# The passage between sublayers of an encoder kernel, reordered by token halves

## The chip, the cores and the metric

One Trainium2 chip, of which one core runs the kernel. The metric is the device time of one execution, in microseconds (us); the median of three runs stands for a kernel.

## The reference, cut to what matters

Two layers with two sublayers each, on 256 tokens of width 2048, all in float32. A sublayer is `x = x + rms_norm(f(rms_norm(x, pre)), post)`, where `f` is a token mixer or a gated MLP with a short convolution:

```
for i in range(DEPTH):
    h = rms_norm(x, p['mix_pre'])
    m = mixer_dilated_gqa(h, ...) if i % 2 == 0 else mixer_mla(h, ...)
    x = x + rms_norm(m, p['mix_post'])
    h = rms_norm(x, p['ffn_pre'])
    x = x + rms_norm(conv_glu(h, ...), p['ffn_post'])
```

So there are four sublayers: mixer 0, FFN 0, mixer 1, FFN 1. The last thing that each of them does is a projection to 2048 columns, its norm, and the addition to `x`; the first thing that the next one does is a projection of the new `x`.

## The kernel before, in words

**Weights.** Every weight is cut into chunks of 128 x 1024 floats, listed in the order of their use (`all_chunks`, L949). SyncE loads a chunk into one of four `raw` buffers (`_load`, L99). `_split` (L106) then makes two parts of it, so that float32 products can be made of products of a shorter type (F32R): ACT copies the chunk to `whi` (L117), and DVE subtracts that from the chunk and writes the rest to `wlo` (L118). There are three buffers of each. `weights` (L129) hands out the next chunk and splits some chunks ahead.

**Inputs.** The input of a sublayer stands in SBUF with features on the partitions: 16 slices k of 128 features, each as a high part and a low part of 256 tokens, side by side. Four tiles `xhl[c]`, c = 0 to 3, hold four slices each (`split`, L319). The parts of one slice are made by one ACT instruction (L516) and one DVE instruction (L517) in `parted_by`, which also multiply by the gain of the norm before. The norm's other factor comes in later, so the square sums of the new `x` (`pre_norm`, L288) aren't needed at once.

**Projections.** `proj_t` (L176) gives features by tokens: for each chunk, which covers two slices k, eight pairs of products, one of 512 columns (the high weights by both parts of x, L186) and one of 256 (the low weights by the high part, L187), into four PSUM banks. `proj_tok` (L191) gives tokens by features: for each chunk and each token half t six products of 512 columns (`mm3`, L172 to L174). The FFN begins with `proj_t`, mixer 1 with `proj_tok`. PSUM has two sets of four banks, tagged `acc` and `at`; both kinds of projection write to `acc` first, the transposes to `at`.

**The passage.** `out_proj` (L332) computes the four blocks of 512 columns of a sublayer's result. Of the last block the last three chunks (`HOLD`) are held: all of token half 0 is finished with them, then all of half 1. When a half is through, `factor(t)` (L369) takes its square sum and root on ACT (L282, L374) and four small steps on DVE (L375 to L379); `add` (L381) adds the scaled result to `x` on DVE. `scaled` (L349) multiplies a block by the norm's gains on DVE. Then TensorE transposes the new `x` (`turns`, L400), 32 transposes of 128 x 128 in all (L405), in pairs of slices that share a PSUM bank, and the parts of each slice are made. The first pair of slices is done at once, the other seven one by one as the next sublayer asks for weights (`rest`, L438, through `follow`, L142). `warm` (L151) puts products of zeros into TensorE's queue, ten and three for each passage. The first chunk of the next sublayer is split in the midst of it (L411). All this runs three times; after the last sublayer (`pre is None`) the result goes out instead.

**What sets the order.** The framework places the instructions on each engine: it goes by its own model of what is ready when, and by the program's order where several are. `behind` puts instructions after a given one on that one's engine; here the seven later pairs and, through `gate`, the splits of weights come behind the first additions.

## Time and profile before

| | us |
|---|---|
| median of three runs | 2072.53 |
| lowest and highest | 2072.30, 2072.53 |
| the profiled execution, its own time | 2072.57 |
| its span in the profile | 2070.8 |

| engine | busy us | share of the span | instructions |
|---|---|---|---|
| TensorE, products (PE) | 2057.9 | 99% | 10977 |
| TensorE, weight loads (PEld) | 1764.1 | 85% | 10977 |
| VectorE (DVE) | 1340.6 | 65% | 2051 |
| ScalarE (ACT) | 1084.6 | 52% | 1695 |

The profile is of one execution. A row of a timeline has the start in us from the span's start, the us until its last instruction ends, the engine, the line of the kernel, what it writes and reads, and how many instructions it merges; in brackets stands how long the engine was idle before it, and what ended that. Products overlap, so a product's length is more than the distance to the next one. A row of groups has the busy time, the mean length in ns, and the idle time before. A row of windows has the stretch, its length, the busy time and instructions of PE, PEld, DVE, ACT and POOL, the granted clock of TensorE as a share of full speed, the share of the DMA engines, and GB/s. The three passages stand at about 323 to 357, 1058 to 1090 and 1323 to 1357 us.

### The profile page before, as it was taken

What the parts mean: (1) busy time and instruction counts of PE and PEld (TensorE: products, weight loads), DVE (VectorE), ACT (ScalarE), POOL (GpSimd) and SP (SyncE); (2) the same over time, 40 slices, a digit from 0 to 9 for tenths busy, and PEclk for the clock granted to TensorE, in tenths of its full rate; (3) what the DMA queues carried; (4) which work ended last, traced back from release to release, by engine and by line L of the source; (5) the groups of instructions that cost most, each with busy time, mean ns of one, the idle gap of its engine ahead of it and who ended that gap; (6) DMA issues with size and microseconds to landing.
All of it is one profiled execution on the core that took longest, in us unless ns stands there. A gap on an engine that the chain in (4) does not pass through costs nothing.

```text
span 2070.8 us, 28951 instructions
## 1 busy us (share of the span) xinstructions
PE 2057.9 (99%) x10977; PEld 1764.1 (85%) x10977; DVE 1340.6 (65%) x2051; ACT 1084.6 (52%) x1695; POOL 0.2 (0%) x4
## 2 busy tenths in 40 slices
PE   9999999999999999999999999999999999999998
PEld 7888888888888888888888998888888888888886
DVE  6877757667667667444466875666766766754444
ACT  6655546555555555344455654555555555544443
POOL 0000000000000000000000000000000000000000
PEclk9999999999999999999999999999999999999999
DMA  8545565666666666666665445566666666666664
GB/s 315 176 153 163 164 200 174 186 193 190 188 192 191 187 192 190 196 198 199 198 186 170 125 129 177 177 188 190 185 195 191 188 191 190 185 200 198 198 194 154
DMA packets 108716, 385.96 MB, mean 186 GB/s; under 512 B 12064, under 2 KB 12576, under 8 KB 108576
## 3 DMA queue, kind: packets, MB, share of 16 engines
q1 hardware_dynamic: 108288, 383.83, 60.6%
q8 instruction: 86, 1.41, 0.3%
q14 instruction: 54, 0.44, 0.1%
q10 hardware_dynamic: 288, 0.28, 0.0%
HBM read 381.96 MB, written 2.10 MB: 185 GB/s over the span
## 4 chain that ended last, share of the span: by engine, by line
PE 98%; DVE 1%; ACT 0%; DMA 0%; issue 0%; DVEq 0%; SPq 0%
PE ps L186 31%; PE ps L172 16%; PE ps L174 16%; PE ps L173 16%; PE ps L187 16%; PE ps L463 1%; PE ps L242 1%; DVE x L383 1%; PE ps L405 0%; DMA raw<-in_w_in 0%; PE ps L790 0%; DVE wlo L118 0%; ACT junk L282 0%; PE ps L238 0%; DVE xhl L517 0%
## 5 line engine op out<-in xcount | busy, mean ns | idle before, releaser
L118 DVE TENSOR_TENSOR wlo<-raw,whi 128x1024 fp32r<-128x1024 f32 (+1 forms) x710 | 867.9, 1223 | 672.1 <-ACT whi L117 670.4
L117 ACT CAST whi<-raw 128x1024 fp32r<-128x1024 f32 (+1 forms) x710 | 745.9, 1052 | 786.5 <-PE ps L174 417.5
L186 PE MATMUL ps<-xhl,whi 128*128 128x512 f32 x2816 | 978.6, 394 | 1.0 <-DVE xhl L517 1.0
L187 PE MATMUL ps<-xhl,wlo 128*128 128x256 f32 x2816 | 779.2, 277 | 0.0
L186 PEld LDWEIGHTS ps<-xhl,whi 128*128 128x128 f32 x2816 | 527.6, 188 | 123.2 <-DVE xhl L517 1.9
L187 PEld LDWEIGHTS ps<-xhl,wlo 128*128 128x128 f32 x2816 | 528.7, 188 | 1.1 <-DVE wlo L118 0.5
L172 PE MATMUL ps<-whi,gh 128*128 128x512 f32 x704 | 273.9, 389 | 0.0
L174 PE MATMUL ps<-whi,gl 128*128 128x512 f32 x704 | 273.9, 389 | 0.0
L173 PE MATMUL ps<-wlo,gh 128*128 128x512 f32 x704 | 273.9, 389 | 0.0
L174 PEld LDWEIGHTS ps<-whi,gl 128*128 128x128 f32 x704 | 132.2, 188 | 27.7
L173 PEld LDWEIGHTS ps<-wlo,gh 128*128 128x128 f32 x704 | 132.2, 188 | 27.4
L172 PEld LDWEIGHTS ps<-whi,gh 128*128 128x128 f32 x704 | 132.2, 188 | 27.1
L172 PE MATMUL ps<-whi,xhl 128*128 128x512 f32 x352 | 138.8, 396 | 1.3 <-ACT whi L117 1.2
L173 PE MATMUL ps<-wlo,xhl 128*128 128x512 f32 x352 | 137.6, 391 | 0.0
L174 PE MATMUL ps<-whi,xhl 128*128 128x512 f32 x352 | 137.1, 391 | 0.0
L172 PE MATMUL ps<-whi,oh 128*128 128x512 f32 x256 | 100.0, 390 | 0.0
L173 PE MATMUL ps<-wlo,oh 128*128 128x512 f32 x256 | 99.7, 389 | 0.0
L174 PE MATMUL ps<-whi,ol 128*128 128x512 f32 x256 | 99.6, 389 | 0.0
L247 ACT COPY half<-ps 128x256 f32<-128x256 f32 x176 | 65.0, 369 | 45.6 <-PE ps L186 36.0
L172 PEld LDWEIGHTS ps<-whi,xhl 128*128 128x128 f32 x352 | 66.0, 188 | 15.1 <-ACT whi L117 1.5
L174 PEld LDWEIGHTS ps<-whi,xhl 128*128 128x128 f32 x352 | 66.0, 188 | 13.9
L173 PEld LDWEIGHTS ps<-wlo,xhl 128*128 128x128 f32 x352 | 66.3, 188 | 13.4 <-DVE wlo L118 0.9
(186 smaller groups left out, 1584.9 us busy)
## 6 DMA issues: line engine op xcount, KB each, us to landing
raw<-in_w_up SPq DMA_DIRECT2D x352, 512.0 KB, 4.1
raw<-in_w_down SPq DMA_DIRECT2D x176, 512.0 KB, 4.2
raw<-in_w_in SPq DMA_DIRECT2D x88, 512.0 KB, 3.8
raw<-in_w_out SPq DMA_DIRECT2D x64, 512.0 KB, 3.9
gb<-in_post SPq DMA_DIRECT2D x16, 256.0 KB, 3.9
raw<-in_w_qn SPq DMA_DIRECT2D x8, 512.0 KB, 3.6
raw<-in_w_kn SPq DMA_DIRECT2D x8, 512.0 KB, 3.6
raw<-in_w_v SPq DMA_DIRECT2D x8, 512.0 KB, 3.6
```

The source lines that it names most:

```text
L117: self.nc.scalar.copy(hi[:, s], raw[:, s])
L118: self.nc.vector.tensor_tensor(out=lo[:, s], in0=raw[:, s], in1=hi[:, s].bitcast(F32), op=ALU.subtract)
L172: mm(ps, lh, rh, start=start, stop=False)
L173: mm(ps, lh, rl, start=False, stop=False)
L174: mm(ps, ll, rh, start=False, stop=stop)
L186: mm(out[i], hi[:, s], x(k), start=k == 0, stop=False)
L187: mm(out[i][:, :T], lo[:, s], x(k)[:, :T], start=False, stop=k == nk - 1)
L242: self.tc.keep_in_program_order(self.nc.tensor.transpose(out, x, self.ident))
L247: self.nc.scalar.copy(b, ps[:, T:])
L383: return nc.vector.scalar_tensor_tensor(out=x, in0=m[c][:, t, s], scalar=r[t], in1=x, op0=ALU.mult, op1=ALU.add)
L463: nc.tensor.matmul(ps[:, i, :], l, r, start=n == 0, stop=n == len(pairs) - 1))
```

## The change

The passage is written anew. What it does:

- The transposes of one slice have a PSUM bank of their own (`turn(k, t)`), where two slices shared one.
- The second half's held chunks get work between them (`between` in `proj_tok`): ahead of the first one the factor, the addition to the first block and the scaling of token half 0; ahead of the second the split of the next sublayer's first chunk; ahead of the third the transposes of slices 0 and 1 for half 0, their parts, and the first half of the second chunk's split (`middle`).
- The next sublayer's first chunk is computed by token halves: what concerns half 0 comes first, then `second()` (the transposes of slices 2 and 3 for half 0, the factor, addition and scaling for half 1, four transposes for half 1, the parts of slices 0 and 1 for half 1, the rest of the second chunk's split, the parts of slices 2 and 3), then half 1. In `proj_tok` that is only an order. In `proj_t` (`by_halves`) the eight pairs of 512 and 256 columns become sixteen of 256 and 128, the wider ones with two runs of 128 columns; the fourth tile's products come after `second()`.
- Both stretches stand in `strict()`: on TensorE, DVE and ACT each instruction is tied behind the one written before it.
- The products of zeros in the passage go away.
- The six later pairs, the next norm's square sums and the splits of weights come behind the half 1 parts of slice 1 on ACT and DVE.
- The scaled results lie two blocks to a tile, in `xm1` and `xm2`; `xhl[1]` is put into `xm3`, `xhl[2]` into `xm1`, `xhl[3]` into `xm2`.

```
+    def _pieces(self, i, parts):
         self._load(i)
...
+        for j in range(parts):
+            s = slice(n * j, n * j + n)
+            self.nc.scalar.copy(hi[:, s], raw[:, s])
+            self.nc.vector.tensor_tensor(out=lo[:, s], in0=raw[:, s], in1=hi[:, s].bitcast(F32), op=ALU.subtract)
+            yield
+
+    @contextmanager
+    def strict(self):
+        traced = self.nc.cur_bb.bb.instructions
+        n = len(traced)
+        yield
+        last = {i.engine: i for i in traced[:n]}
+        for i in traced[n:]:
+            if i.engine in self.ordered and i.engine in last:
+                self.tc.add_manual_dep(i, last[i.engine].name, ..., reason="strict")
+            last[i.engine] = i
...
+    def by_halves(self, out, x):
+        mm = self.nc.tensor.matmul
+        hi, lo = self.weights(self.at + 1)
+        both = lambda a: a.rearrange("p (a t) -> p a t", a=2)
+        def products(t, tiles):
+            ts = slice(t * P, (t + 1) * P)
+            for i in tiles:
+                for k in range(2):
+                    s = slice(k * 512 + i * P, k * 512 + (i + 1) * P)
+                    mm(both(out[i])[:, :, ts], hi[:, s], both(x(k))[:, :, ts], start=k == 0 and t == 0, stop=False)
+                    mm(out[i][:, ts], lo[:, s], x(k)[:, ts], start=False, stop=False)
+        second, self.second = self.second, None
+        with self.strict():
+            products(0, range(3))
+            second()
+            products(0, [3])
+            products(1, range(4))
+        self.tick()
...
     def proj_tok(...)
+            if self.second is not None:
+                second, self.second = self.second, None
+                w = self.weights(self.at + 1)
+                with self.strict():
+                    chunk(c, 0, w)
+                    second()
+                    chunk(c, 1, w)
+                self.tick()
+                continue
...
-            for t in range(2):
-                for c in range(n - hold, n):
-                    chunk(c, t, ws[c - n + hold])
+            with self.strict() if between else ExitStack():
+                for t in range(2):
+                    for c in range(n - hold, n):
+                        if t == 1 and between:
+                            between[c - n + hold](out)
+                        chunk(c, t, ws[c - n + hold])
...
     def out_proj(...)
-        add(0, 0, full)
-        add(1, 0, full)
-        add(2, 0, full)
-        self._split(self.at)
-        turns(0, 0)
-        turns(1, 0)
-        factor(1)
-        self.warm(10)
-        self.xhl = [None] * 4
-        last = add(0, 1, slice(0, 256))
...
+        def half(t):
+            ts = slice(t * P, (t + 1) * P)
+            parts = [self.split(k, tp[k][:, ts], pre, ts) for k in range(2)]
+            return parts[1]
+        def ahead(out):
+            nonlocal ps
+            ps = out
+            factor(0)
+            add(0, 0, full)
+            scaled(3, 0)
+        def middle(out):
+            turn(0, 0)
+            turn(1, 0)
+            half(0)
+            next(pieces)
+        def second():
+            turn(2, 0)
+            turn(3, 0)
+            factor(1)
+            add(0, 1, full)
+            scaled(3, 1)
+            for k in range(4):
+                turn(k, 1)
+            self.gate = half(1)
+            next(pieces)
+            for k in range(2, 4):
+                self.split(k, tp[k], pre)
+            self.led, self.lead = 2, rest()
         def rest():
+            for p in range(2, 8):
+                with self.behind(self.gate):
+                    c, h = divmod(p, 2)
+                    for t in range(2):
+                        if h == 0:
+                            add(c, t, full)
+                    for k in range(2 * p, 2 * p + 2):
+                        turn(k, 0)
+                        turn(k, 1)
+                        self.split(k, tp[k], pre)
                 self.led = p + 1
                 yield True
+        pieces = self._pieces(self.at + HOLD + 1 + (nk // 2 - HOLD), 2)
+        self.proj_tok(nk, parts, order, hold=HOLD, between=(ahead, lambda out: self._split(self.at), middle))
+        self.second = second
```

101 lines of the change are left out of this document (42 added, 59 removed).

## The prediction

> **What bounds the kernel now.** I read the page first (span, busy shares, the chain), then the timeline of TensorE, DVE and ACT where one sublayer passes to the next, then the groups by line in windows around that place, then the granted clock.
>
> ```profile
> span 2070.8 us, 28951 instructions
> PE 2057.9 (99%) x10977; PEld 1764.1 (85%) x10977; DVE 1340.6 (65%) x2051; ACT 1084.6 (52%) x1695; POOL 0.2 (0%) x4
> PE 98%; DVE 1%; ACT 0%; DMA 0%; issue 0%; DVEq 0%; SPq 0%
> ```
>
> TensorE is the bound, and the chain leaves it for about 1% of the span. So a change that adds and removes no product of the reference can win only what TensorE loses, and this one touches three places: the passages from the first mixer, the first FFN and the second mixer. The profiled execution took 2072.57 us, 1.77 more than its span; the median of the runs is 2072.53, so both stand for the same. Here is TensorE in the first passage:
>
> ```profile
> 326.81 0.39 PE L173 MATMUL ps<-wlo,oh 128*128 128x512 f32 x1
> 327.04 0.40 PE L174 MATMUL ps<-whi,ol 128*128 128x512 f32 x1
> 327.27 0.60 PE L405 MATMUL ps<-ident,x 128*128 128x128 f32 x4
> 327.71 1.25 PE L156 MATMUL ps<-zeros 128*128 128x256 bf16 x10
> 328.80 0.60 PE L405 MATMUL ps<-ident,x 128*128 128x128 f32 x4
> 329.82 0.44 PE L405 MATMUL ps<-ident,x 128*128 128x128 f32 x2 [0.42 <-DVE x L383]
> 330.09 0.49 PE L156 MATMUL ps<-zeros 128*128 128x256 bf16 x3
> 331.34 0.50 PE L186 MATMUL ps<-xhl,whi 128*128 128x512 f32 x1
> 332.79 0.50 PE L186 MATMUL ps<-xhl,whi 128*128 128x512 f32 x1 [0.48 <-DVE xhl L517]
> 338.15 0.63 PE L186 MATMUL ps<-xhl,whi 128*128 128x512 f32 x2
> ```
>
> The last product of the old sublayer starts at 327.04 and the first of the new one at 331.34; in between stand transposes (L405) and 13 products of zeros that compute nothing (L156). A wide product takes a slot of 0.23 us (326.81 to 327.04), a transpose or a filler 0.109 (ten fillers from 327.71 to 328.80). What the passage loses is its length less the work in it:
>
> ```profile
> L186 PE MATMUL ps<-xhl,whi 128*128 128x512 f32 x16 | 5.9, 413 | 0.5 <-DVE xhl L517 0.5
> L187 PE MATMUL ps<-xhl,wlo 128*128 128x256 f32 x16 | 4.3, 286 | 0.0
> L405 PE MATMUL ps<-ident,x 128*128 128x128 f32 x19 | 3.3, 278 | 0.5 <-DVE x L383 0.4
> ```
>
> That is the window from 327.45 to 338.15, so from the first transpose (327.27) to the 17th L186 there are two chunks (16 pairs) and 19 transposes. In the steady stretch:
>
> ```profile
> L186 PE MATMUL ps<-xhl,whi 128*128 128x512 f32 x58 | 20.2, 394 | 0.0
> ```
>
> 58 pairs in 20 us (window 360 to 380) is 0.345 a pair. So 10.88 - 16 x 0.345 - 19 x 0.109 = **3.29 us lost**, 1.42 of it fillers. The third passage shows the same counts (window 1327.7 to 1338.38) and I take 3.29 for it. For the second (window 1062.65 to 1090.0; its first transpose is at 1062.45) stand:
>
> ```profile
> L172 PE MATMUL ps<-whi,xhl 128*128 128x512 f32 x32 | 12.9, 409 | 0.0
> L173 PE MATMUL ps<-wlo,xhl 128*128 128x512 f32 x31 | 12.2, 393 | 0.0
> L174 PE MATMUL ps<-whi,xhl 128*128 128x512 f32 x31 | 11.9, 395 | 0.0
> L405 PE MATMUL ps<-ident,x 128*128 128x128 f32 x32 | 5.2, 274 | 0.4 <-DVE x L383 0.4
> ```
>
> 27.6 - 94 x 0.227 - 32 x 0.109 = 2.75. Together 9.3 us, 0.45% of the time: the ceiling of any gain here. About 0.2%, 4.1 us, is what a measurement of this kernel can tell from no change, so nearly half of all the loss would have to go for a visible gain.
>
> **The change part by part.** What holds the passage is a chain that the change keeps: square sum, root, factor, add, transpose, split. Its durations, in the order of the first passage:
>
> ```profile
> 323.38 0.60 ACT L282 ACTIVATE junk<-ps 128x512 bf16<-128x512 f32 x1 [3.02 <-PE ps L174]
> 324.10 0.29 ACT L374 ACTIVATE post<-post,part 128x1 f32<-128x1 f32 x1
> 324.74 1.06 ACT L117 CAST whi<-raw 128x1024 fp32r<-128x1024 f32 x1 [0.34 <-PE ps L174]
> 325.13 2.08 DVE L383 SCALAR_TENSOR_TENSOR x<-m,postr,x 128x512 f32<-128x512 f32 x3
> 327.13 1.22 DVE L118 TENSOR_TENSOR wlo<-raw,whi 128x1024 fp32r<-128x1024 f32 x1
> 330.80 0.48 DVE L517 SCALAR_TENSOR_TENSOR xhl<-ps,gains,xhl 128x256 fp32r<-128x256 f32 x1
> 332.65 0.68 DVE L350 TENSOR_TENSOR m<-ps,gb 128x512 f32<-128x512 f32 x1
> 330.29 0.47 ACT L516 ACTIVATE xhl<-ps,gains 128x256 fp32r<-128x256 f32 x1 [1.19 <-PE ps L405]
> ```
>
> From the end of a token half's last product (about 323.34, just before the square sum's 323.38) to its first add (325.13) are 1.79 us; three adds take 2.08, one about 0.75 and 0.67 when queued; a transpose takes about 0.33 to its result, and the parts follow on ACT and DVE. A wait costs about 0.05 (L516 ends at 330.76, L517 starts at 330.80).
>
> *First half.* The half's add ends at 325.88, as now, and the third held chunk of the second half would start six slots before 327.27, at 325.91, so the two transposes put ahead of it wait 0.04. They delay the second half's end by 0.26 + 0.1 for the refill: last slot 327.68 instead of 327.27. On DVE the scaling (0.60 queued, since starts come some 0.08 before the previous end) and the weights' low part (1.13 queued) stand ahead of the half parts: 325.80, 326.40, then 327.53. Half parts of 128 columns are not in the trace with L516 and L517; the nearest rows are
>
> ```profile
> L512 DVE TENSOR_TENSOR hl<-y,hl 128x128 fp32r<-128x128 f32 x2 | 0.5, 284 | 0.0
> L511 ACT CAST hl<-y 128x128 fp32r<-128x128 f32 x2 | 0.5, 296 | 0.0
> ```
>
> so 0.28 to 0.48 on DVE; I take 0.35, and 0.37 on ACT. The first half's second low part is done at 328.14, the first at 327.88: the new products start at 327.94, a stall of 0.26.
>
> *The products by halves.* In the two FFN passages 16 pairs of 256 and 128 columns take the place of 8 of 512 and 256. The 256 slot is 0.345 - 0.23, about 0.118. For 128 columns the nearest row is
>
> ```profile
> 1136.43 1.40 PE L238 MATMUL ps<-ident_r,hl 128*128 128x128 f32 x15
> 1137.67 0.59 PE L463 MATMUL ps<-qk 128*128 128x256 f32 x3
> ```
>
> 15 slots in 1.24 us, 0.083 each, the same width and type, though a transpose. The bounds are half the 256 slot (0.059) and all of it. 16 x (0.118 + 0.083) - 8 x 0.345 = 0.46 more; bounds 0.07 and 1.02. The second mixer takes its first chunk by halves anyway: nothing.
>
> *Second half.* Its square sum starts at 327.88; 1.79 later comes the add, 329.68 to 330.43. Six pairs from 327.94 end at 329.25, two transposes at 329.47, and then TensorE, in its pinned order, **waits for the add until 330.49: 1.0 us**, with every product behind it. (On DVE the add, the scaling and the half parts stand behind the factor's wait for ACT's root; on ACT the half parts and the second piece stand behind the square sum. TensorE is who waits for all of them.) Four transposes end at 330.98; the fourth tile's bank comes free with the scaling at 331.09 (0.1 more); its two pairs end at 331.59; the second half's parts are ready at 331.60 and 331.87, and the chunk ends at 333.36. Chunk two's weights (second piece by 332.5) and parts (332.9, 333.3) are there. So chunk three can start at 333.36 + 2.76 + 0.44 = 336.56, with 12 transposes done: 336.56 - 327.27 - 5.52 - 1.31 = 2.46 lost.
>
> *Chunk three.* Here DVE and ACT have no slack:
>
> ```profile
> 331.30:338.20 6.90, 6.42 (x39) 5.36 (x37) 6.78 (x12) 6.87 (x17) 0.00 (x0) 1.00 0.28 91
> ```
>
> 6.78 and 6.87 us busy of 6.90 (DVE, ACT). The change moves the next norm's square sums behind the half parts and the low halves of the second chunk's weights into the passage. DVE is through with k = 3 at 333.25, then come two adds (334.6), the third chunk's low weights (1.13) and two parts (0.4 each), 336.5 in all if ACT's copy is in time; ACT is through with k = 3 at 332.8, and if two square sums of some 0.7 go ahead of its 1.06 copy, the low weights start at 335.3 and the last part comes at 337.3. So 0 to 0.45 us of waiting (its first product needs only the first part); I take 0.2, as no row tells the order. Loss 2.66, gain **0.63 for each FFN passage**.
>
> *The second passage*, in the same frame: six wide products end at 329.05, two transposes at 329.27, the wait lasts to 330.73. It is 0.25 longer, because the memset is now pinned into DVE's order ahead of the second half's factor:
>
> ```profile
> 1081.02 0.27 DVE L739 MEMSET kr<- 64x256 f32 x1
> ```
>
> The second half can begin with its high parts at 331.53 and ends at 333.0; chunk three at 336.2. Loss 336.2 - 327.27 - 24 x 0.227 - 1.31 = 2.18, with 0.2 for chunk three 2.4: gain **0.35**.
>
> *Without a price.* The end of the last sublayer keeps its order. Paired m tiles and the new places of the split input add no instruction. The chunk cut into pieces was loaded before, and its buffer is freed sooner than now; no DMA moves and SP's and POOL's queues are passed by nothing. The fillers' 1.42 us are no gain by themselves: they lie in time that TensorE waits.
>
> Sum: 2 x 0.63 + 0.35 = 1.6 us, 2072.57 - 1.6 = **2070.9**.
>
> One thing speaks against the 0.118: the halved FFN products read and write two runs of 128 columns with a gap, and every product of the rows above has one run. The sum keeps 0.118, since the columns are as many; the third rival has the other end. The Trainium skill says in PSUM — Partial Sum Buffer (Specifications) that any non-contiguous access pattern slows matmuls significantly, without a figure; no run here shows it, and by it the sum would come out as in that rival.
>
> **The rivals.**
>
> *More is hidden.* If the narrow slot is 0.059, the first stall goes and chunk three never waits, losses fall to about 1.9 (FFN) and 1.85: 2 x 1.4 + 0.9 = 3.7 gained, 2068.9, at best 2067.9. Against it stands the 1.0 us wait, which is pure latency. 0.14.
>
> *DVE takes over.* The low weights of chunk three behind the parts of k = 4 and 5 cost one L118 slot, 1.13, in each passage in place of the 0.2: 2070.9 + 2.8 = 2073.7 at worst, 2072.3 if it strikes in half of them. For it: the row of 331.30, and the program order. Against: where DVE was full, parts and weights were interleaved. 0.18. That the pins change nothing real and the time stays at 2072.5: 0.04.
>
> *Two-run products are slow.* If a two-run 256-column product costs the slot of the 512 (0.23), the FFN passages pay 16 x 0.11 = 1.8 each: 2070.9 + 3.6 = 2074.5, slower than before. It decides from 0.04 us a product (16 x 0.04 = 0.63). 0.07.
>
> *The clock falls without the fillers.*
>
> ```profile
> 2065.00:2066.00 1.00, 0.00 (x0) 0.00 (x0) 1.00 (x2) 0.00 (x0) 0.00 (x0) 1.00 0.19 72
> 2066.00:2067.00 1.00, 0.00 (x0) 0.00 (x0) 1.00 (x3) 0.00 (x0) 0.00 (x0) 0.79 0.43 170
> 2067.00:2068.00 1.00, 0.00 (x0) 0.00 (x0) 0.70 (x2) 0.00 (x0) 0.00 (x0) 0.50 0.97 375
> 2062.00:2063.00 1.00, 0.79 (x4) 0.33 (x2) 1.00 (x3) 0.18 (x1) 0.00 (x0) 1.00 0.49 190
> 1.08 4.66 PE L156 MATMUL ps<-zeros 128*128 128x256 bf16 x24 [1.08 <-DVE zeros L941]
> ```
>
> At the end TensorE stops at 2062.8 and the granted clock (before the DMA share) halves at 2066.6, 3.8 us later; at the start 24 fillers take 4.66 us where 2.6 would do, so one cold spell costs 2 us. Three make 2070.9 + 6 = 2077. The longest stretch without products is 1.85 us here, 2.5 in the second passage; it decides from 3.8. 0.05. The page TensorE: Matmul & The Clock Gate (Part 1) puts the window at about 3.4 us, and its Part 4 says that transposes do not count as activity; that agrees with the trace's 3.8, and by it too the stretches are too short.
>
> **How the numbers follow.** The forecast has 0.52 and for itself 2069.9 to 2072.0 (the narrow slot's and chunk three's bounds). The range 2068.6 to 2073.2 leaves out the clock, the two-run products, the worst of DVE and the best of the hiding, some 0.2. Faster by over 0.2% (below 2068.4) is the better half of the first rival, 0.07; slower (above 2076.7) the clock and an extreme of the two-run products, 0.05; the rest, 0.88, is within.
>
> **What would show it.** Right: no L156 in the passages; six pairs from about 0.3 us after the old sublayer's end; a wait of about 1.0 us on DVE's add at the second half's transposes in all three passages; some 0.08 a narrow product; the clock at 1.00. Wrong: no such wait (more gained), a 256-column slot above 0.16, the third chunk waiting over 0.5 us for L118 or L517, or the clock below 1.00.

## The result, and the profile after

The changed kernel took 2090.71 us (median of 5 runs, 2090.33 to 2091.96), the kernel before 2072.53 in the same session. The ratio is 1.0068, with a 95% interval of 1.0042 to 1.0093. It is 18 us slower; 2070.9 was forecast, with 2073.2 as the upper end. One of the five runs of the kernel before took 2081.61, and that turned out to matter. Two runs in this document with a mean granted clock of 0.73 and 0.56, at 2616.76 and 3446.24 us, are left out of every count.

The profiled run took 2090.33 us. Its page shows the same picture as before, only longer: TensorE busy 99%, its share of the chain 98%, and a granted clock at 9 tenths or more in every slice.

```profile
span 2088.5 us, 28973 instructions
PE 2073.1 (99%) x10970; PEld 1772.3 (85%) x10970; DVE 1340.2 (64%) x2057; ACT 1082.7 (52%) x1704; POOL 0.2 (0%) x4
PEclk9999999999999999999999999999999999999999
PE 98%; DVE 1%; ACT 0%; DMA 0%; issue 0%; DVEq 0%; SPq 0%
```

The busy time of TensorE rose by 15.2 of the 17.7 us that the span grew by (2057.9 to 2073.1), with 7 instructions fewer. So for the most part instructions became dearer, and it is not waits that grew. To find where, cut the span at points that both kernels have: the root of a factor, the four products that broadcast the norm's factor over the partitions (`prer`, L309 before, L370 after; they stand between an FFN's first and second up projection), the first down product, the first product of `w_kr`. From root to broadcast the first passage takes 32.58 us before and 32.69 after, the third 32.53 and 32.68; from root to `w_kr` the second takes 53.85 and 53.77. All other stretches agree within 0.3 us but one: from the broadcast products to the first down product each FFN takes 466.37 us before and **475.33** after. Two times 8.96 is 17.9, the whole loss, and none of it lies in a passage. In those stretches TensorE makes nothing but up projections. Here are their wide products in the 400 us from 400 to 800, first before, then after (L211 is what was L186):

```profile
L186 PE MATMUL ps<-xhl,whi 128*128 128x512 f32 x1155 | 400.4, 394 | 0.0
```

```profile
L211 PE MATMUL ps<-xhl,whi 128*128 128x512 f32 x1133 | 400.4, 399 | 0.0
```

There is no idle time in either row, and yet 1155 pairs fit into the time before and 1133 after: 346.7 and 353.4 ns a pair. The starts of the single products show two rhythms that keep themselves up. In the short one, pairs of 343 and 350 ns alternate, or all take 347; in the long one 350, 350 and 361 follow each other. Both occur in both kernels, the long one for some us in the passage before too, and TensorE's clock is 1.00 in both. One FFN has 1344 pairs behind the broadcast products: 1344 x 6.7 ns is 9.0 us, the step by which that one run of the kernel before was longer.

The passage itself, in the rows of TensorE after (to be held against those of the prediction; the root is at 323.81 here, 0.29 earlier than before):

```profile
327.10 0.40 PE L196 MATMUL ps<-whi,ol 128*128 128x512 f32 x1
327.64 0.39 PE L227 MATMUL ps<-xhl,whi 128*128 128x256 f32 x1
...
329.10 0.40 PE L467 MATMUL ps<-ident,x 128*128 128x128 f32 x2
330.17 0.66 PE L467 MATMUL ps<-ident,x 128*128 128x128 f32 x4 [0.67 <-DVE x L447]
330.77 0.39 PE L227 MATMUL ps<-xhl,whi 128*128 128x256 f32 x1
...
332.35 0.33 PE L227 MATMUL ps<-xhl,whi 128*128 128x256 f32 x1
332.51 0.22 PE L228 MATMUL ps<-xhl,wlo 128*128 128x128 f32 x1
332.57 0.33 PE L227 MATMUL ps<-xhl,whi 128*128 128x256 f32 x1
...
333.27 0.29 PE L467 MATMUL ps<-ident,x 128*128 128x128 f32 x1
334.31 0.55 PE L467 MATMUL ps<-ident,x 128*128 128x128 f32 x3 [0.75 <-DVE x L447]
334.61 0.48 PE L211 MATMUL ps<-xhl,whi 128*128 128x512 f32 x1
...
337.87 0.48 PE L211 MATMUL ps<-xhl,whi 128*128 128x512 f32 x1
```

No filler stands there any more. The new products start at 327.64, 0.54 after the start of the last old one; the wait for DVE's add ahead of the second half's transposes is there; and a second wait stands ahead of chunk two, which the prediction had not seen.

### The profile page after: what moved, and what is told of

Its sections match the earlier page's. It is cut to its first block, busy times and chain, and to the rows that moved or that the text cites. A ratio compares the mean times of both kernels' runs of the same rounds, so it can differ in the third digit from the quotient of the medians.

```text
span 2088.5 us, 28973 instructions
## 1 busy us (share of the span) xinstructions
PE 2073.1 (99%) x10970; PEld 1772.3 (85%) x10970; DVE 1340.2 (64%) x2057; ACT 1082.7 (52%) x1704; POOL 0.2 (0%) x4
## 4 chain that ended last, share of the span: by engine, by line
PE 98%; DVE 1%; ACT 0%; DMA 0%; issue 0%; DVEq 0%; SPq 0%
PE ps L211 31%; PE ps L212 16%; PE ps L194 16%; PE ps L195 16%; PE ps L196 16%; PE ps L535 1%; PE ps L302 1%; DVE x L447 0%; PE ps L467 0%; DMA raw<-in_w_in 0%; DVE xhl L589 0%; PE ps L862 0%; DVE wlo L127 0%; PE ps L298 0%; ACT xhl L588 0%
## 5 line engine op out<-in xcount | busy, mean ns | idle before, releaser
L211 PE MATMUL ps<-xhl,whi 128*128 128x512 f32 x2800 | 990.8, 399 | 0.0
L212 PE MATMUL ps<-xhl,wlo 128*128 128x256 f32 x2800 | 787.1, 281 | 0.0
L211 PEld LDWEIGHTS ps<-xhl,whi 128*128 128x128 f32 x2800 | 526.9, 188 | 129.9
```

The lines of the kernel that those rows point to most:

```text
L211: mm(out[i], hi[:, s], x(k), start=k == 0, stop=False)
L212: mm(out[i][:, :T], lo[:, s], x(k)[:, :T], start=False, stop=k == nk - 1)
```

## The experiments

Eighteen experiments were run; two of them repeat an earlier kernel, to see how its runs spread. The words "fast" and "slow rhythm" in the expectations mean 346.7 and 353.3 ns a pair.

**First: places or rhythm?** The change also moved tiles in SBUF (the split input by `X_TAGS`, two m blocks in one tile). The theory "places" says that the operands' addresses cost the 6.7 ns; the theory "rhythm" says that the same products can run in two ways, and that the moment at which TensorE goes on behind something inserted decides. The places alone, put into the kernel before:

```
+X_TAGS = 0, 3, 1, 2
-            self.xhl[c] = self.act.tile([P, 4, 2, T], F32R, tag=f"xm{c}", name=f"xhl{c}")
+            self.xhl[c] = self.act.tile([P, 4, 2, T], F32R, tag=f"xm{X_TAGS[c]}", name=f"xhl{c}")
-            m.append(self.act.tile([P, 2, 512], F32, tag=f"xm{c + 1}", name=f"m{c}"))
+            place(c)        # two m blocks in one tile, as in the changed kernel
```

> The kernel before with the changed kernel's places in SBUF alone (results two blocks to a tile in xm1 and xm2, the split input's tiles in xm0, xm3, xm1, xm2); the passage and its order stay. Theory of places (each pair of the FFN takes 353.3 ns in place of 346.7 because its operands lie elsewhere): about 2090, both FFNs at 353. Theory of rhythm (TensorE has two rhythms for the same products, 346.7 and 353.3 a pair; which one it falls into is settled by the moment at which it goes on after the last inserted products, and it keeps it): the moments are those of before, so 2072.5 and 346.7; a flip of one FFN would add 9.0.

It took 2072.95 us beside 2073.05 for the kernel before, and 1154 pairs fit into the 400 us:

```profile
L187 PE MATMUL ps<-xhl,whi 128*128 128x512 f32 x1154 | 400.1, 394 | 0.0
```

So the new places alone don't bring the long rhythm. This is one run; that they don't bring it within the changed order either is shown further down, where that kernel, with its new places, runs in the short rhythm. The reverse, the old places in the changed kernel, was not run.

Then something was inserted on purpose: at the head of every up projection one product of zeros, 0, 16, 32 ... 240 columns wide in turn, in the changed kernel and in the kernel before.

```
         out = [self.psum(tag) for _ in range(4)]
+        n = 16 * (self.taps % 16)
+        self.taps += 1
+        if n:
+            mm(out[0][:, :n], self.zeros[:, :P], self.zeros[:, :n], start=True, stop=True)
```

> The changed kernel with one product of zeros ahead of each of the 44 up projections, of 0, 16, 32 to 240 columns in turn (the first three of them follow each other, then it starts over); it is overwritten, so nothing is computed otherwise. Theory of rhythm: a product of another length shifts the moment at which TensorE goes on, so within one run some projections go at 346.7 ns a pair and others at 353.3, changing only at the inserted products; the time lies between 2073 and 2091 (about 4 us for the products themselves included). Theory of places: all at 353.3, about 2095.

> The same 42 products of zeros put into the kernel before. Theory of rhythm: here too both rhythms appear, changing only at the inserted products, so the time goes up by more than the products' 4 us, to between 2077 and 2094. Theory of places: all at 346.7, about 2076.

They took 2084.93 and 2085.25 us: the slower kernel gained nearly 6, the faster lost 12, and both came out alike. Between two inserted products lie 64 pairs. Within an FFN each such stretch, from one inserted product's start to the next one's, took about 22.3 or 22.7 us and kept its rhythm to its end. Three stretches of 20 us of the changed kernel, behind 80, 96 and 176 columns (L216 is the wide product):

```profile
L216 PE MATMUL ps<-xhl,whi 128*128 128x512 f32 x58 | 20.6, 401 | 0.0
```

```profile
L216 PE MATMUL ps<-xhl,whi 128*128 128x512 f32 x59 | 20.5, 394 | 0.0
```

```profile
L216 PE MATMUL ps<-xhl,whi 128*128 128x512 f32 x59 | 20.5, 392 | 0.0
```

Behind 160 columns and more the rhythm was short and flat each time; behind 16 to 144 it depended on the width and on the rhythm ahead, and the long rhythm followed whenever 343 and 350 had alternated ahead. So one inserted product settles the rhythm of all that follows. Theory "rhythm" stands so far.

In the third variant the two wide products of a tile go ahead of its two narrow ones:

> The changed kernel with another order within the up projections' chunks: the two products of 512 columns of a tile, then its two of 256, in place of one by one. Theory of rhythm: the two rhythms belong to an order, so another order has another mean, most likely not 353.3 for a pair; the time then moves by several us either way. Theory of places: the operands lie where they did and each product is as slow as before: 2090.7, 353.3 a pair.

It took 2077.42 us, 348.3 ns a pair in both FFNs (the stretch to the first down product is 468.6 us). Run again ten times, to see whether this order has a second rhythm:

> The changed kernel with both hi products of a tile ahead of its two lo products, as run before, now many times. If this order has only one rhythm (348.3 ns a pair in both FFNs of the one trace), every run is at 2077.4 within 0.6 us. If it has two as well, runs stand some us apart in steps.

Half of the runs lay at 2076.9 to 2077.2, the others at 2078.5 to 2078.8. No run shows a step of 9.0, so this order has one rhythm; the 1.7 us are another matter, which comes last. The order costs 2.2 us an FFN against the short rhythm and saves 6.7 against the long.

**Second: can a product be put in to set the rhythm?**

```
-    def proj_t(self, nk, x, tag):
+    def proj_t(self, nk, x, tag, tap=0):
+        if tap:
+            mm(out[0][:, :tap], self.zeros[:, :P], self.zeros[:, :tap], start=True, stop=True)
-                pv = self.proj_t(KD, x, "at")
+                pv = self.proj_t(KD, x, "at", 256 if gi == 0 else 0)
```

> The changed kernel with one zero product of 256 columns at the head of the second up projection of each FFN, just behind the four broadcast products. Rhythm theory: in the kernel with many zero products every width from 160 columns on was followed by the fast rhythm, so both FFNs now run at about 346.7 ns a pair; from the broadcast products to the first down product 466.5 us instead of 475.3 in each FFN, and 2072.6 us in all (2090.3 less 2 x 9.0, plus 0.3 for the two products). Rival, a standing cause (something in the changed program that makes each of its products dearer whatever went before): 353.3 ns a pair as before, 2090.6 us.

This failed: 2090.9 us (median of 10), though 4 of the 10 runs lay one step lower, at 2082. The rule "160 columns and more give the short rhythm" does not hold right behind the broadcast products. The kernel before with 16 columns at the same place:

> The kernel before with one zero product of 16 columns at the same place. Rhythm theory: in the kernel before with many zero products this width was followed by the slow rhythm in the first FFN, so the first FFN takes 475.3 us from the broadcast products to the first down product and the time is 2081.6 us; if the second FFN is caught in the same way, 2090.6 us. Rival, a standing cause in the changed program: the kernel before stays at 466.4 us in both, 2072.6 us.

It took 2090.57 us, with 475.4 us in both FFNs. That is what the theory asked for, but the session also ran the kernel before 19 times, and those runs stand at three levels: 11 at 2072.5 to 2072.9, 6 at 2081.4 to 2081.7, 2 at 2090.5. **Each execution settles the rhythm of each FFN anew, and a kernel only sets the odds.** All 104 runs of the kernel before, over all sessions: 66 with both FFNs short, 35 with one long, 3 with both, so one FFN in five is long (41 of 208). The changed kernel again:

> The changed kernel itself, unaltered, run many times. Runs of the kernel before have by now stood at three levels, 2072.5, 2081.5 and 2090.5 us, one step of 9.0 for each FFN in the slow rhythm, so which rhythm an FFN gets is settled anew in each execution and a kernel only sets the odds. Entry theory: the odds hang on the rhythm in which the products run as the four broadcast products come; they come into the fast rhythm in every trace of the changed kernel and leave the slow one behind, so nearly all runs at 2090.5. Luck theory: one coin for all kernels, about one FFN in four slow as in the kernel before, so runs at all three levels and most at 2072.8.

Of 7 runs 4 had both FFNs long, 2 one, 1 none; with the first five, 20 FFNs of 24 are long. The odds went from 0.20 to 0.83. The median of five runs hides that: it names only the commonest level. In the mean the kernel before takes 2076.1 us (104 runs) and the changed one 2088.1 (12).

**Third: what turns the odds?** A first attempt put 64 zero columns 8 pairs ahead of the broadcast products in the first FFN and 16 pairs ahead in the second, so that they should meet another rhythm:

```
+            if c == flip:          # 7 in the first FFN, 6 in the second; first up projection
+                mm(self.psum('at')[:, :64], self.zeros[:, :P], self.zeros[:, :64], start=True, stop=True)
```

> The changed kernel with one zero product of 64 columns ahead of the last chunk of the first up projection in the first FFN (8 pairs ahead of the broadcast products), and ahead of the last chunk but one in the second (16 pairs). Entry theory: every product of 48 to 144 columns that came into the fast rhythm left the slow one behind, so the broadcast products now come into the slow rhythm, as in the one profile in which they left the fast one behind; at least one of the two FFNs is fast in most runs, and the median lies at 2081.6 or 2072.9. Luck theory: the same spread as the changed kernel itself in the same session.

8 of 10 runs had one long FFN, median 2081.95. In the profile the second FFN meets the broadcast products in the long rhythm and leaves them in the short one; the first meets them in the flat short one and leaves them in the long one. So what stands ahead of the broadcast products matters. With all 13 profiles in which nothing else is inserted there, 26 FFNs:

```
ahead of the broadcast products        behind them
long                                   short in 9 of 9
343 and 350 in turn, 343 last          short in 8 of 8
343 and 350 in turn, 350 last          long in 5 of 5
flat 347                               long in 2 of 2
not yet settled                        short in 2 of 2
```

In every trace of the changed kernel itself they come in the third way. The row can be read in the profile: a pair of 350 ns has lengths of 0.40 and 0.28 us, one of 343 has 0.39 and 0.27. The changed kernel:

```profile
355.80 0.39 PE L211 MATMUL ps<-xhl,whi 128*128 128x512 f32 x1
356.03 0.28 PE L212 MATMUL ps<-xhl,wlo 128*128 128x256 f32 x1
356.15 0.40 PE L211 MATMUL ps<-xhl,whi 128*128 128x512 f32 x1
356.38 0.28 PE L212 MATMUL ps<-xhl,wlo 128*128 128x256 f32 x1
356.50 0.61 PE L370 MATMUL ps<-ident,prer 128*128 128x128 f32 x4
```

If that is the cause, one pair more or less between the last disturbance and the broadcast products must turn the outcome round, and two must not. Nothing else is changed here than the pair ahead of which the broadcast products stand:

```
                 for kk in range(2):
+                    if (c, i, kk) == spot:      # two new arguments of proj_t: spot, call
+                        call()
-                pg = self.proj_t(KD, x, "acc")
+                pg = self.proj_t(KD, x, "acc", ((7, 3, 1), (7, 3, 1))[layer] if gi == 0 else None, lambda: self.finish(norm))
```

> The changed kernel with the broadcast products of each FFN ahead of the last pair of the first up projection, one pair earlier, and nothing else moved. Phase theory: the fast rhythm alternates pairs of 343 and 350 ns; in every trace of the changed kernel the broadcast products come behind the same one of the two and leave the slow rhythm behind, while in the traces of the kernel before that come in fast they come behind the other one and leave the fast rhythm. One pair earlier they meet the other phase: most FFNs fast, the median at 2073.1, with the odds turned round (about one FFN in five slow). Luck theory (the spot doesn't matter, only what the passage left behind): the spread of the changed kernel itself, about four FFNs in five slow, median 2090.6 or 2081.8.

All ten runs had both FFNs short: median **2072.82** us, 2072.53 to 2074.45. Ahead of the broadcast products now stands the other pair, and 1155 pairs fit into 400 us again:

```profile
356.22 0.39 PE L213 MATMUL ps<-xhl,whi 128*128 128x512 f32 x1
356.45 0.27 PE L214 MATMUL ps<-xhl,wlo 128*128 128x256 f32 x1
356.56 0.60 PE L372 MATMUL ps<-ident,prer 128*128 128x128 f32 x4
```

```profile
L213 PE MATMUL ps<-xhl,whi 128*128 128x512 f32 x1155 | 400.4, 394 | 0.0
```

One pair earlier in the first FFN, two in the second (`(7, 3, 0)`):

> The same with one pair earlier in the first FFN and two pairs earlier in the second. Phase theory: two pairs are a whole period, so the second FFN stays slow in most runs while the first turns fast: median 2081.9, and in the profile 466.4 us from the broadcast products to the first down product in the first FFN and 475.3 in the second. If any move away from the boundary between projections helps, both are fast, 2073.1. Luck theory: as for the changed kernel, 2090.6 or 2081.8.

8 of 10 runs had one long FFN, two had none: median 2081.75. The profiled run is one of the two; its second FFN met the broadcast products in the long rhythm. That the long one is the second FFN in the other eight is likely, as the first has the edit with which it was short in ten of ten, but it is not shown: the total doesn't tell which FFN was long. So the half of the test by which two pairs must not turn the outcome rests on that count alone. And the kernel before, one pair earlier:

> The kernel before with its broadcast products one pair earlier. Phase theory: those of its FFNs that come into the fast rhythm now leave it slow, so the level of 2072.7, which holds over half of its runs, becomes rarer and the median goes to 2081.5 or 2090.3. If the spot doesn't matter, or if any move helps: 2072.7 still the commonest.

9 of 10 runs had one long FFN: median 2081.7. In the profiled one it is the second, which meets the broadcast products in the flat rhythm. The first meets them four pairs behind an irregular place and stays short. So the same one-pair move sets the changed kernel right and the kernel before wrong: the place of the broadcast products in the stream turns the odds, with both passages left as they are. That the alternation of 343 and 350 is what does it is shown for the changed kernel; in the traced run of the kernel before neither FFN had that alternation ahead, so there the expected number came by another row of the table.

**Fourth: why did the passages bring nothing?** The wait ahead of chunk two (333.27 to 334.31 above) could be the transposes' place, which stand ahead of the chunk's products. Asked for behind its first tile instead:

```
-            hi, lo = self.weights()
+            hi, lo = self.weights(follow=False)
             for i in range(4):
+                if i == 1:
+                    self.follow()
```

> The changed kernel with the transposes of slices 4 and up asked for behind the first tile's products of each chunk and no longer ahead of the chunk. If the wait of 1.0 us ahead of chunk two comes from their place in TensorE's order alone, the stage from the first root to the broadcast products falls from 32.69 us to 31.7 to 31.9 in both FFNs; if DVE is the bound there, the wait goes over to chunk three and the stage stays above 32.5. The rhythm theory doesn't say which rhythm the FFNs get, only that it is one of two: 466.4 or 475.3 us from the broadcast products to the first down product, so 2070.7, 2079.7 or 2088.7 us in all. The standing cause says 2088.7.

> The last kernel with the zero product of 256 columns as well. Rhythm theory: both FFNs fast whatever the passages did, 2070.9 us (2072.6 less 2 x 0.85). Standing cause: 2088.9 us.

They took 2076.1 us (one run, in whose trace the clock was halved for 3.4 us twice, at the start and in the second passage, which the last part takes up) and 2084.0 (median of ten, at all three levels). The passages got longer: 33.00 and 32.97 us from root to broadcast. TensorE starts chunk two at once and then waits inside it, for an add that DVE now makes behind a weight difference of 1.2 us. Rows of the second kernel, TensorE and then DVE:

```profile
335.80 0.44 PE L472 MATMUL ps<-ident,x 128*128 128x128 f32 x2 [0.72 <-DVE x L452]
```

```profile
333.86 1.21 DVE L127 TENSOR_TENSOR wlo<-raw,whi 128x1024 fp32r<-128x1024 f32 x1
335.00 1.41 DVE L452 SCALAR_TENSOR_TENSOR x<-m,postr,x 128x512 f32<-128x512 f32 x2
```

With the adds kept ahead of the weights (`rest` yields once behind the adds and once behind the transposes):

> The changed kernel with the transposes of slices 4 and up asked for behind the first tile of a chunk, and this time with DVE's residual adds kept where they were, ahead of the next chunk's weight split. Moving the transposes alone left the stage from the first root to the broadcast products at 33.0 us, because the adds fell behind a weight split of 1.2 us. If the wait ahead of chunk two is the transposes' place alone, the stage now falls from 32.69 to 31.8; if DVE is the bound all along, it stays within 0.2 of 32.69. What the FFNs do after that is not foretold by either: 466.4 or 475.4 us each.

The passages took 32.50 and 32.63 us instead of 32.69: 0.2 at most of the 0.9 that the wait was worth. (The ten runs stand at all three levels, median 2081.43.) So DVE holds the chunk back and not TensorE's order. If so, taking work off DVE there must shorten the passage. GpSimd was given half of chunk two's weight difference, on top of the one-pair move and of the fillers told of below:

```
+            e = self.nc.gpsimd if parts == 2 and j == 1 and self.led == 0 else self.nc.vector
-            self.nc.vector.tensor_tensor(out=lo[:, s], ...)
+            e.tensor_tensor(out=lo[:, s], ...)
```

> The kernel with the broadcast products one pair earlier and the zero products in the second passage, and with the second half of chunk two's weight difference (128x512, 0.6 us on DVE) made by GpSimd, which is idle. If DVE is what the end of a passage hangs on, add(1,1) comes 0.6 us earlier, the wait ahead of chunk two falls from 0.75 to about 0.15, and the stage from the first root to the broadcast products (32.35 us with the broadcast one pair earlier) goes to 31.75 in both FFNs: 2071.5 us in all. If the transposes' place on TensorE is what costs, or if GpSimd's product comes later than chunk two needs it, the stage stays at 32.35 or above: 2072.7 or more.

> The same with the transposes of slices 4 and up behind the first pairs of a chunk and the adds kept early. That edit alone brought 0.2 us. If DVE was what held it, it now brings its full wait: the stage goes to 31.4 or 31.5 us, 2070.9 in all if both FFNs stay fast. If something else holds it, no better than the last kernel. The phase in which the broadcast products come may change with the passage, in which case runs stand at steps of 9.0 above.

The first took **2072.24** us, with 2072.05 to 2072.31 in eleven runs; ratio to the kernel before 0.9985 (0.9971 to 0.9999). The passage is 32.01 and 32.07 us, 0.3 less than the 32.36 and 32.35 without GpSimd, and the wait fell from 0.75 to 0.40, about half of what was expected of both:

```profile
334.35 0.55 PE L472 MATMUL ps<-ident,x 128*128 128x128 f32 x3 [0.40 <-DVE x L452]
```

```profile
332.13 1.61 POOL L128 TENSOR_TENSOR wlo<-raw,whi 128x512 fp32r<-128x512 f32 x1 [331.69 <-ACT whi L126]
```

```profile
333.30 1.00 DVE L452 SCALAR_TENSOR_TENSOR x<-m,postr,x 128x512 f32<-128x512 f32 x1
```

Of the 0.6 us taken from DVE 0.26 came back, since the add took 1.00 us beside GpSimd where it takes 0.74, and so in all three passages. The Trainium skill says in GPSIMD Engine Reference (Specifications) that GpSimd shares SBUF interfaces with VectorE and that they contend when a DVE instruction has two SBUF inputs, as this add has. This row agrees; but the add before it, from 331.85 to 332.59, lies beside GpSimd's first 0.46 us and took its usual 0.74, so it is not shown that this contention is the cause. The second kernel, with the transposes moved too, took 2073.41 (2073.28 to 2073.52) and 32.61 us a passage: the first transposes of its second chunk no longer wait, but the first pairs of the next two chunks start some 0.2 to 0.3 us late (at 336.94 and 340.65). The gain that was expected did not come, and what holds those pairs is open.

**Last: the 1.7 us.** In the changed kernel and the seven variants with its second passage that ran ten times, 22 of 82 runs lie 1.2 to 1.8 us above one of the levels, and just these 22 have a mean granted clock of 0.998, the others 0.999; of the 104 runs of the kernel before, none. Two traces show such a run, that of the variant with the transposes moved and that of the one with the adds kept early. The latter: TensorE in the second passage, then windows (the granted clock is the figure before the DMA share):

```profile
1072.69 0.39 PE L197 MATMUL ps<-whi,xhl 128*128 128x512 f32 x1
1072.92 0.38 PE L470 MATMUL ps<-ident,x 128*128 128x128 f32 x2
1074.84 0.66 PE L470 MATMUL ps<-ident,x 128*128 128x128 f32 x4 [1.54 <-DVE x L450]
1075.62 0.50 PE L195 MATMUL ps<-whi,xhl 128*128 128x512 f32 x1
```

```profile
1075.00:1076.00 1.00, 0.87 (x6) 0.55 (x5) 0.78 (x3) 0.80 (x3) 0.00 (x0) 1.00 0.60 215
1076.00:1077.00 1.00, 1.00 (x4) 0.87 (x3) 1.00 (x3) 1.00 (x4) 0.00 (x0) 0.52 0.32 115
1077.00:1078.00 1.00, 1.00 (x3) 0.73 (x3) 1.00 (x3) 1.00 (x3) 0.00 (x0) 0.50 0.54 121
1079.00:1080.00 1.00, 1.00 (x5) 0.82 (x4) 1.00 (x1) 0.56 (x1) 0.00 (x0) 0.78 0.70 270
```

For 2.7 us (1072.92 to 1075.62) TensorE has nothing but six transposes, and at about 1076.0 its clock halves for 3.4 us, when the products are already running again; half of that is the 1.7 us. In the trace of the changed kernel the same gap leaves the clock at 1.00. The Trainium skill says in TensorE: Matmul & The Clock Gate (Part 1) that the window in which activity is counted runs freely and is about 3.4 us long, and that the clock goes down after one idle window. The traces bear out the free-running window: in all of them the clock changes at whole multiples of 3.413 us, counted from its first rise. On this grid the gap lies whole within one step in three of the twelve traces that have it. Two of the three are those with a dip, which begins with the next step; in the third the gap ends 0.02 us before its step does. In the nine traces where the gap straddles two steps the clock stays at 1.00. An estimate from these figures: a gap of 2.70 us that falls at random lies within one step in (3.413 - 2.70) / 3.413, 21% of the runs, beside 22 of 82. But a step with a gap of 2.7 us in it is not idle as a whole, so the gap that is enough is shorter than by the page, and here the measurement decides. To test whether the gap is the cause, zero products were put into the gap:

```
                     chunk(c, 0, w)
+                    for _ in range(12):
+                        self.nc.tensor.matmul(out[1][:, :T], self.zeros[:, :P], self.zeros, start=True, stop=True)
                     second()
```

> The first of these with twelve zero products of 256 columns in the second passage, ahead of the transposes that stand before its second half, in a bank that isn't in use yet; they take 1.3 us of a wait of 1.8. A part of the runs of the changed kernel and its variants lies 1.6 to 1.8 us above its level, and one profiled so shows TensorE's clock at 0.50 for about 3.3 us behind that wait. If idling there brings the clock down, no run of this kernel lies 1.6 above its level, the time is otherwise that of the first (2073.1 when both FFNs are fast), and the second passage stays within 0.1 of 53.75 us from root to first kr product. If the dip comes from elsewhere, it is as frequent as before, about a run in four.

```profile
1064.11 1.49 PE L267 MATMUL ps<-zeros 128*128 128x256 bf16 x12
1065.43 0.38 PE L471 MATMUL ps<-ident,x 128*128 128x128 f32 x2
1066.03 0.66 PE L471 MATMUL ps<-ident,x 128*128 128x128 f32 x4 [0.22 <-DVE x L451]
```

The median was 2072.74 us in nine runs, 2072.51 to 2072.87, ratio 0.9983 (0.9966 to 0.9999), and the second passage stayed at 53.75. No run of the three kernels with these fillers lies that far above its level, 0 of 31, where 3 of 10 did without them. So the fillers of the kernel before did work in the second passage.

## Why the prediction was wrong

**The step that failed** is one that the prediction made without a word. It took 0.345 us for a pair from a row of the steady stretch, used it to find the loss of the passages, and ended at 2072.57 - 1.6: that the 1344 pairs of each FFN outside the passages keep their time was taken for granted. They went to 353.4 ns in both FFNs, 2 x 8.96 us. It rested on one window of 20 us; the single starts of the kernel before show 353 ns a pair from 344.7 to the broadcast products at 356.69 and 346.7 behind them, in the very trace that the prediction read. None of the rivals covered it; those slower than before, at 2073.7, 2074.5 and 2077, had other causes.

Why the broadcast products come in another phase is seen in the order. The kernel before has an irregular place five pairs ahead of them in both FFNs, where the planner put two wide products in a row; the changed kernel has none.

```profile
354.09 0.75 PE L186 MATMUL ps<-xhl,whi 128*128 128x512 f32 x2
354.68 0.40 PE L187 MATMUL ps<-xhl,wlo 128*128 128x256 f32 x2
```

That this place is what gives the kernel before its better odds is argued, not shown: it was not taken out by itself.

Point by point, in the frame of the first passage, shifted by the 0.29 that all of it came earlier:

- *First half.* The first new product was forecast at 327.94, so 327.65 when shifted, behind a stall of 0.26. It came at 327.64, 0.31 behind the end of the last old slot (327.10 + 0.23). Right.
- *The wait for the add.* "TensorE waits for the add until 330.49: 1.0 us": shifted, 330.20; it lasted to 330.17. Right, also in the third passage. In the second it was 1.54 of idle time instead of 0.67, longer as said; the pinned memset is 0.27 of that.
- *Narrow products.* 0.201 a pair was forecast. The starts of the pairs that follow each other without a break lie about 0.23 apart, 0.17 for the 256 columns in two runs and 0.06 for the 128 (the rows from 332.35 to 332.57 show one pair). So the 128-column term lay at its lower bound and the 256-column term some 0.05 above the value taken, past the 0.16 that the prediction named as a sign of being wrong: 0.03 a pair, 16 x 0.03 = 0.5 us. Half of the pairs lie in time that is waited for anyway, and the first chunk ends at 333.27, 0.20 later than the 333.07 of the shifted forecast. The rival of two-run products took 0.23 for a slot where 0.17 was measured, and whether it had the cause is open: the two runs were never tried alone, and another cause fits as well. Each product needs a weight load of its own, and the loads (PEld, the figure behind PE's) stand without a gap there, 13 in 1.35 us, where the usual pairs leave them idle for some 14%:

```profile
331.85:333.20 1.35, 1.35 (x13) 1.35 (x13) 1.35 (x4) 1.35 (x3) 0.00 (x0) 1.00 0.47 164
400.00:401.40 1.40, 1.40 (x10) 1.21 (x9) 0.89 (x1) 1.12 (x3) 0.00 (x0) 1.00 0.66 222
```

  The Trainium skill says in PSUM — Partial Sum Buffer (Specifications) that any non-contiguous access pattern slows matmuls significantly. The 0.17 against 0.118 would agree, but because of the loads these rows can't show it.
- *Chunk three.* A wait of 0.2 was forecast there; instead chunk two is held up by 0.9 (333.27 to 334.61, less four transposes), because transposes of slices 4 and 5 stand ahead of it in TensorE's order and need an add for which DVE has no time. By chunk three 16 transposes are done, not 12, so by the prediction's own working the loss up to there is 337.87 - 326.98 - 5.52 - 16 x 0.109 = 3.6, where 2.46 stood: 0.9 and 0.2 of the difference are these two terms. That is 0.3 more than the 3.29 of the kernel before, of which 0.11 is left at the broadcast products. That DVE had "no slack" was read rightly from its row; what was missed is who waits for it first.
- *The sum of the passages.* Forecast gains of 0.63, 0.35 and 0.63; measured, to the broadcast products or to `w_kr`, -0.11, +0.08 and -0.15. (The loss of the second passage is 2.72 by the prediction's own rows, 1090.0 - 1062.45 less the work, and not 2.75; nothing hangs on that.)
- *The clock.* Forecast not to fall, since it was thought to need 3.8 us without products. In the profiled run it didn't. In about a quarter of the runs it does, in the second passage, at a gap of 2.7 us, and costs 1.7 and not 2. That rival, with its chance of 0.05, was under-rated.

With the broadcast products one pair earlier the same change takes 2072.82 us, inside the forecast range. That it lies there is no success of the sum: the passages brought none of the 1.6 us forecast, and the range was wide enough for no change. The 18 us are not lost in the passages.

## What to carry to other kernels

Before a row's time per instruction is carried from one kernel to another, look whether the steady stretch has it everywhere, and in every run: here a stream of the same products with no idle time has two lengths 2% apart, and what stands ahead of one small inserted product picks one for the next 466 or 475 us. When a change costs time far from where it was made, cut both traces at common points before explaining anything, and run both kernels often enough to see levels, since the median of five names only one of them. An expected gain of a few tenths of a us needs a list of everyone who waits for the busiest helper engine, not only of the wait that is removed.

## What the runs showed of the hardware

- The same alternation of 512- and 256-column products runs at 346.7 or at 353.4 ns a pair with the clock at 1.00, and either holds for a thousand pairs and more. What makes the two rhythms inside TensorE stays open: lengths differ by about 7 and 11 ns, and no view shows what a product waits for there. An order of two wide and two narrow products has one rhythm, 348.3 ns.
- In a stream of 256- and 128-column products in turn, the wider ones reading and writing two runs of 128 columns, a pair takes 0.23 us, 0.17 and 0.06; 256 columns in one run, between products of 512, take 0.118. Whether the two runs or the weight loads make the difference is open.
- GpSimd takes 1.61 us for a difference of 128x512 that DVE makes in 0.60 to 0.69. An add of DVE beside its last 0.44 us takes 1.00 us in place of 0.74, one beside its first 0.46 us the usual 0.74.
- A gap of 2.7 us without products, with six transposes in it, brought the clock down to 0.50 for 3.4 us in two of twelve traces, beginning some 3 us after the gap's start, when products were running again; by their times and mean clocks it did so in 22 of 82 runs. The clock changes on a grid of 3.413 us that runs through the whole execution, and whether a gap of this length counts hangs on where it falls on the grid.

The version with the broadcast products one pair earlier, fillers in the second passage and GpSimd's share is the best of all: 2072.24 us, 0.4 below the commonest level of the kernel before, 3.9 below its mean, and in none of its runs a long FFN.
